# Low parts of the weights by an adding DMA on POOL, and the forget logs broadcast from device memory

## The chip, the cores and the metric

One core of one Trainium2 chip runs the whole program. The metric is the device time of the program in microseconds (us). Engines are named as the profile names them: PE is TensorE, DVE is VectorE, ACT is ScalarE, POOL is GpSimd, SP is SyncE, which here only issues DMAs. Each engine works through its own instructions in order.

## What is computed

Two layers over 512 tokens of width 1024. A layer projects the normalized input with one wide matrix, mixes the tokens by three branches of four heads (retention, gated linear attention, "forgetting" attention), joins them by gated projections, and ends with a gated feed-forward part with a short convolution. The forgetting attention adds a running sum of log forget gates to its logits:

```python
log_f = jax.nn.log_sigmoid(f_logit.astype(F32))
cum = jnp.cumsum(log_f, axis=1).transpose(0, 2, 1)
logits = jnp.einsum('bihd,bjhd->bhij', q[:, q0:q1], k[:, :q1]).astype(F32) * d ** -0.5
logits = logits + cum[:, :, q0:q1, None] - cum[:, :, None, :q1]
```

All inputs are float32. Modulation vectors (shift, scale, gate) come from `c_act @ w_ada`, a matrix of 6 x 1024 columns per layer.

## The kernel before

Activations lie transposed, features on the 128 partitions and the 512 tokens along the row, so one matmul has 128 rows of weights and 512 columns of tokens. To keep precision with the fp32r matmul type, every product is made of three matmuls (`mm3`, L238 to L241): rounded weight times rounded activation, rounded weight times the activation's low part, and the weight's low part times rounded activation.

All weights are laid out on the host in `wall`, 302 units of 128 x 1024 float32 (512 KB), in the order of use. A unit feeds 24 matmuls of 512 columns in most stages. It passes three steps: `dma_to` issues its load on SP into a tile `wr` (4 buffers, shared with the rows `ar` of `w_ada`), `prep_hi` rounds it on ACT into `wh` (L122, 5 buffers), and `prep_lo` makes the low part `wl` (5 buffers) as raw minus rounded on DVE (L131). `ahead` calls these for the units up to `depth` ahead of the one in use; `depth` is 3 or 4, and 1 inside a head group.

The order of the program on each engine is the order in which the code is written: there is no scheduler. `col_block` runs one unit; smaller work (norms of the heads, attention items) is queued as generators and advanced by `tick`, twice per unit, in PE steps and evacuation steps.

Stages that the text speaks of, with the time of the first layer:

- start: loads of `x`, the first units and the columns of `w_ada` that the first normalization needs (`ad`, 16 pairs); PE is kept busy with warm-up matmuls.
- first head group (`head_group`, not halved; 20 to 63 us): k runs over the 8 blocks of the input, one unit per k feeds 8 banks. For each k, `h_a` makes `ht` on DVE (L314) and `hhi` on ACT (L315), `h_b` makes `hlo` on DVE (L320); the modulation columns `mod` for the k after are summed on DVE (L333) and finished on POOL (L339 to L343). The matmuls are L363: `wh` by `hhi`, then `wl` by `hhi`, then `wh` by `hlo`.
- the three other head groups (at 576, 940 and 1498 us) work in halves of 256 tokens, with 6 banks; their normalization is finished while they run (`sums` with a power on POOL, L294; `spread`). They start out of `tail_blocks`, which prepares units ahead at fixed steps (`S1`, `S3`).
- projections and heads: `qk_evac` copies the banks (L510, L512), `qk_norm` normalizes them, `gates_item` makes the log forget gates, sums them up on 4 partitions (`cum`, L589) and sends them to all 128 partitions (`cumb`, L597). `fox_item` subtracts `cumb` from the scores (`fl`, L653); its matmuls are L649 (`fs`), L665 (`fT`) and L675 (`fo`).
- during the gated projections and the feed-forward part of layer 0, one `ar` load on SP and one sum on DVE (L151) accompany most units, 80 in all.

Of the kernel before, what the change touches and what calls it, by code (L numbers as in the profile page):

```python
# [7 lines left out]
F32 = mybir.dt.float32  # L8
F32R = mybir.dt.float32r
BF16 = mybir.dt.bfloat16  # L10
AF = mybir.ActivationFunctionType
ALU = mybir.AluOpType
# [13 lines left out]
S = 512  # L26
NH = 4
# [27 lines left out]
def tile_hybrid_layers(ctx: ExitStack, tc: tile.TileContext, xT, cvec, wall, wada, par, a2, cst, tabs, out):  # L55
# [5 lines left out]
    wh_p = ctx.enter_context(tc.tile_pool(name="wh", bufs=5))  # L61
    wl_p = ctx.enter_context(tc.tile_pool(name="wl", bufs=5))
    sm_p = ctx.enter_context(tc.tile_pool(name="sm", bufs=2))
    psm = ctx.enter_context(tc.tile_pool(name="psm", bufs=8 - NA, space=PS))
    psa = ctx.enter_context(tc.tile_pool(name="psa", bufs=NA, space=PS))

    V, A, G, T, Q = nc.vector, nc.scalar, nc.gpsimd, nc.tensor, nc.sync

    def slot(nm, dt=F32):
        return slots.tile([128, S], dt, tag="slot", name=nm)  # L70
# [6 lines left out]
    def free(n=1):  # L77
        live[0] -= n

    def ba(nm="ba"):  # L80
        live[0] += 1
        return psa.tile([128, S], F32, tag="a", name=nm)
# [3 lines left out]
    def cc(n):  # L86
        o, w = CC[n]
        return C[:, o:o + w]
# [3 lines left out]
    def pp(l, n, i=0, w=1):  # L92
        o, _ = PC[n]
        return P_l[l][:, o + i:o + i + w]
# [12 lines left out]
    raw, wgt = {}, {}  # L107
# [18 lines left out]
    def prep_lo(u):  # L126
        while state["lo"] < min(u, NU):
            i = state["lo"]
            hi = wgt[i][0]
            lo = wl_p.tile([128, UW], F32R, tag="wl", name="wl")  # L130
            V.tensor_tensor(lo, raw.pop(i), hi.bitcast(F32), op=ALU.subtract)  # L131
            wgt[i] = (hi, lo)
            state["lo"] += 1

    def prep_to(u):
        prep_hi(u)
        prep_lo(u)
# [210 lines left out]
    def head_group(l, sec, nm, h, half):  # L348
# [18 lines left out]
        if not half:  # L367
# [3 lines left out]
            ada0_sum(1, 1)  # L371
            prep_hi(2)
            prep_lo(1)
            ada0_sum(1, 0)
            h_b(l, sec, 0, t, h, FULL)
            for kc in range(KD):
                if kc + 1 < KD:
                    t = h_a(l, sec, kc + 1, nm.rb, h, FULL)
                    prep_hi(kc + 3)
                    prep_lo(kc + 2)  # L380
                    if kc + 2 < KD:
                        ada0_sum(kc + 2, 1)
                        ada0_sum(kc + 2, 0)
                    h_b(l, sec, kc + 1, t, h, FULL)
                mms(kc, None)
                dma_to(kc + 5)
                if kc + 4 < KD:
                    ada0_load(kc + 4)
# [83 lines left out]
    def layer(l, nm, h):  # L472
# [80 lines left out]
        def gk_evac(b, o):  # L553
            if b == 0:
                R["gk"] = [slot("gk"), slot("gk")]
                R["sml"] = sm_p.tile([128, NB, 20], F32, tag="sml", name="sml")
            A.copy(R["gk"][b // 2][:, (b % 2) * 256:(b % 2) * 256 + 256], o[:, 0:256])
            V.tensor_copy(R["sml"][:, b, :], o[:, 256:276])
            if b == NB - 1:
                queue.append((gates_item(), 1))  # L560
                queue.append((la_item(0), 1))
                queue.append((la_item(1), 1))
                for hh in range(NH):
                    for ib in range(NB):
                        queue.append((fox_item(hh, ib), 1 + ib // 2))

        def gates_item():
            yield P1
            ps = ba("smT")
            for b in range(NB):  # L570
                T.transpose(ps[0:20, b * 128:b * 128 + 128], in_=R["sml"][:, b, :], identity=cc("ident"))
            yield E_
            gl = slot("glrT")
            V.memset(gl[0:32, :], 1.0)
            V.tensor_copy(gl[0:20, :], ps[0:20, :])
            free()
            e = slot("fe")
            m = slot("fm")
            fb = pp(l, "foxb")[0:4]
            A.activation(e[0:4], gl[0:4], AF.Abs, bias=fb)  # L580
            A.activation(e[0:4], e[0:4], AF.Exp, scale=-1.0)
            A.activation(e[0:4], e[0:4], AF.Ln, bias=cc("one")[0:4])
            V.tensor_scalar(m[0:4], gl[0:4], fb, 0.0, op0=ALU.add, op1=ALU.min)
            yield E_
            R["glrT"] = gl
            V.tensor_tensor(m[0:4], m[0:4], e[0:4], op=ALU.subtract)
            V.memset(e[0:4], 1.0)
            cum = slot("cum")
            V.tensor_tensor_scan(cum[0:4], e[0:4], m[0:4], 0.0, op0=ALU.mult, op1=ALU.add)  # L589
            yield P1  # L590
            pc = ba("cumc")
            for b in range(NB):
                T.transpose(pc[:, b * 4:b * 4 + 4], in_=cum[0:4, b * 128:b * 128 + 128],
                            identity=cc("ident")[0:4, 0:4])
            cb = [slot("cumb") for _ in range(NH)]
            for hh in range(NH):
                Q.dma_start(out=cb[hh], in_=cum[hh:hh + 1, None, :].to_broadcast([1, 128, S]))  # L597
            yield E_
            R["cumc"] = sm_p.tile([128, 16], F32, tag="cumc", name="cumc")
            V.tensor_copy(R["cumc"], pc[:, 0:16])  # L600
            free()
            R["cumb"] = cb
# [403 lines left out]
    with tc.manual_schedule():  # L1006
# [24 lines left out]
        for k in range(KD):  # L1031
            square_acc(k, acc)
            if k in (K0, K1):
                i = int(k == K1)
# [172 lines left out]
```

## Time and profile before

| | before |
|---|---|
| median of three runs | 1866.81 us (1865.39 to 1867.63) |
| span of the profiled execution | 1864.4 us |
| DMA queue q1 (issued by SP) | 65290 packets, 218.57 MB, 38.5% of 16 engines' time |
| mean DMA rate | 118 GB/s |
| mean granted TensorE clock | 0.986 |

The profiled execution has no time of its own on the page besides its span; the median of the runs stands 2.4 us above it. The page gives busy time by engine, a row of 40 slices of 46.6 us with the busy share in tenths, the chain of work that ended last, groups of instructions by line (count, busy time, mean ns, then the idle time ahead of them and what ended it), and DMA issues with the time to landing. In timelines a row is start, length, engine, line, operation, output <- inputs, and in brackets the idle time before it with what ended that. A view of windows gives busy time, granted clock and DMA share in chosen stretches.

### The profile page before, as it was taken

The page shows a single profiled execution, that of the slowest core. Times are in us where ns is not written, and L with a number is a line of the kernel's source. Part 1 is how long each engine was busy: PE and PEld are TensorE (multiplying, and loading weights), DVE is VectorE, ACT ScalarE, POOL GpSimd, SP SyncE. Part 2 cuts the span into 40 slices and gives each one's busy share as a digit, 9 for nine tenths or more (in the row PEclk, how much of TensorE's full clock was granted, in tenths as well). Part 3 has the DMA queues.
Part 4 walks back from the last instruction along what each step waited for, and adds up shares of the span by engine and source line. Part 5 has one row for each costly group of instructions (what it writes and reads, how often), then busy time and mean ns, then how long its engine had stood idle before and what let it go on. Part 6 is the DMA issues. An engine that isn't in the chain of part 4 may idle for free.

```text
span 1864.4 us, 22544 instructions
## 1 busy us (share of the span) xinstructions
PE 1805.6 (97%) x8991; PEld 1508.4 (81%) x8991; DVE 1002.1 (54%) x1515; ACT 672.2 (36%) x1124; POOL 85.4 (5%) x101
## 2 busy tenths in 40 slices
PE   9995999999999999999999869999999999999999
PEld 6874878888889888888898648788888898888887
DVE  7663754565665676764257347544434466444321
ACT  4662433332333443332148334333323244333210
POOL 3210100000000000000001001000000000000000
PEclk9997999999999999999999979999999999999999
DMA  9346222345552465554223542322222233322231
GB/s 335 126 55 92 69 91 90 125 158 192 169 181 86 152 236 181 191 193 158 79 69 124 38 98 69 102 91 69 90 95 98 79 102 102 100 93 94 71 121 55
DMA packets 65395, 220.01 MB, mean 118 GB/s; under 512 B 7263, under 2 KB 7689, under 8 KB 65290
## 3 DMA queue, kind: packets, MB, share of 16 engines
q1 hardware_dynamic: 65290, 218.57, 38.5%
q8 instruction: 71, 1.16, 0.3%
q14 instruction: 34, 0.28, 0.0%
HBM read 214.34 MB, written 2.10 MB: 116 GB/s over the span
## 4 chain that ended last, share of the span: by engine, by line
PE 92%; DMA 3%; DVE 2%; SPq 2%; ACT 1%; issue 0%; POOL 0%; DVEq 0%; ACTq 0%
PE bm L239 23%; PE bm L241 23%; PE bm L240 23%; PE bm L363 4%; PE ga L363 4%; PE bm L534 3%; DMA wr<-wall 3%; PE bm L535 2%; PE bm L536 2%; SPq L597 2%; PE ro L795 1%; PE rs L783 1%; PE fs L649 1%; PE fo L675 1%; PE go L761 0%; ACT wh L122 0%
## 5 line engine op out<-in xcount | busy, mean ns | idle before, releaser
L131 DVE TENSOR_TENSOR wl<-wr,wh 128x1024 fp32r<-128x1024 f32 x302 | 368.8, 1224 | 360.3 <-ACT wh L122 360.0
L239 PE MATMUL bm<-hhi,wh 128*128 128x512 f32 x1296 | 520.3, 401 | 0.0
L241 PE MATMUL bm<-hhi,wl 128*128 128x512 f32 x1296 | 505.5, 390 | 0.0
L240 PE MATMUL bm<-hlo,wh 128*128 128x512 f32 x1296 | 504.9, 390 | 0.0
L122 ACT CAST wh<-wr 128x1024 fp32r<-128x1024 f32 x302 | 314.5, 1047 | 358.5 <-PE bm L240 232.2
L239 PEld LDWEIGHTS bm<-hhi,wh 128*128 128x128 f32 x1296 | 243.4, 188 | 54.4 <-issue 4.2
L240 PEld LDWEIGHTS bm<-hlo,wh 128*128 128x128 f32 x1296 | 243.5, 188 | 53.0 <-issue 2.9
L241 PEld LDWEIGHTS bm<-hhi,wl 128*128 128x128 f32 x1296 | 243.2, 188 | 51.9
L239 PE MATMUL bm<-fah,wh 128*128 128x512 f32 (+1 forms) x374 | 141.0, 377 | 0.0
L240 PE MATMUL bm<-fal,wh 128*128 128x512 f32 (+1 forms) x374 | 140.8, 377 | 0.0
L241 PE MATMUL bm<-fah,wl 128*128 128x512 f32 (+1 forms) x374 | 140.8, 377 | 0.0
L534 PE MATMUL bm<-wh,hhi 128*128 128x512 f32 (+1 forms) x256 | 99.7, 389 | 0.0
L151 DVE SCALAR_TENSOR_TENSOR ar<-ar,cact 128x1024 f32<-128x1024 f32 x80 | 97.5, 1218 | 0.0
L535 PE MATMUL bm<-wl,hhi 128*128 128x512 f32 (+1 forms) x256 | 95.5, 373 | 0.0
L536 PE MATMUL bm<-wh,hlo 128*128 128x512 f32 (+1 forms) x256 | 95.1, 371 | 0.0
L240 PEld LDWEIGHTS bm<-fal,wh 128*128 128x128 f32 x374 | 70.3, 188 | 13.0
L241 PEld LDWEIGHTS bm<-fah,wl 128*128 128x128 f32 x374 | 70.3, 188 | 13.0
L239 PEld LDWEIGHTS bm<-fah,wh 128*128 128x128 f32 x374 | 70.3, 188 | 12.7
L904 DVE SCALAR_TENSOR_TENSOR x<-bm,mod,x 128x512 f32<-128x512 f32 (+1 forms) x39 | 25.5, 655 | 101.3 <-PE bm L241 101.3
L942 DVE TENSOR_TENSOR fu<-fu,bm 128x512 f32<-128x512 f32 x42 | 28.9, 688 | 69.6 <-PE bm L241 59.8
L867 ACT ACTIVATE mg<-bm,der 128x512 f32<-128x512 f32 x48 | 32.9, 685 | 82.4 <-PE bm L241 82.4
L941 ACT ACTIVATE fu<-fu 128x512 f32<-128x512 f32 x44 | 27.8, 632 | 93.9 <-DVE fu L939 93.9
(213 smaller groups left out, 2406.3 us busy)
## 6 DMA issues: line engine op xcount, KB each, us to landing
wr<-wall SPq DMA_DIRECT2D x302, 512.0 KB, 3.6
ar<-wada SPq DMA_DIRECT2D x80, 512.0 KB, 3.9
ad<-wada SPq DMA_DIRECT2D x32, 256.0 KB, 6.0
x<-xT SPq DMA_DIRECT2D x8, 256.0 KB, 4.2
cumb<-cum SPq DMA_DIRECT2D x8, 256.0 KB, 30.2
dec<-tabs SPq DMA_DIRECT2D x8, 256.0 KB, 4.3
out<-x SPq DMA_DIRECT2D x8, 256.0 KB, 2.1
cos<-tabs SPq DMA_DIRECT2D x2, 256.0 KB, 4.0
```

The lines of the kernel that those rows point to most:

```text
L122: A.copy(hi, raw[i])
L131: V.tensor_tensor(lo, raw.pop(i), hi.bitcast(F32), op=ALU.subtract)
L151: V.scalar_tensor_tensor(out=r, in0=r, scalar=1.0, in1=cact, op0=ALU.mult, op1=ALU.mult, accum_out=mod[l][:, b:b + 1])
L239: T.matmul(o, lhsT=wh, rhs=ah, start=first, stop=False)
L240: T.matmul(o, lhsT=wh, rhs=al, start=False, stop=False)
L241: T.matmul(o, lhsT=wl, rhs=ah, start=False, stop=last)
L363: T.matmul(banks[f % GB][:, ts], lhsT=got[f // 8][wi][:, (f % 8) * 128:(f % 8) * 128 + 128], rhs=h[kc][hi][:, ts], start=kc == 0 and hf != ...
L534: T.matmul(o, lhsT=h[k][0][:, bs], rhs=wh[:, ws], start=k == 0, stop=False)
L535: T.matmul(o, lhsT=h[k][0][:, bs], rhs=wl[:, ws], start=False, stop=False)
L536: T.matmul(o, lhsT=h[k][1][:, bs], rhs=wh[:, ws], start=False, stop=k == KD - 1)
L597: Q.dma_start(out=cb[hh], in_=cum[hh:hh + 1, None, :].to_broadcast([1, 128, S]))
L867: A.activation(g, o, AF.Tanh, scale=0.5, bias=der[l][:, i * 8 + j:i * 8 + j + 1])
```

## The change

Two edits. The low part of a unit is no longer a subtraction on DVE: ACT writes the negated unit into the fp32r tile `wl` (which rounds it, so that the tile holds the negated rounded unit), and a DMA issued on POOL adds the raw unit, read once more from device memory, onto it. And the log forget gates are first stored to a tile in device memory by a DMA on POOL, and broadcast from there by four DMAs on POOL, where SP broadcast them from one SBUF partition each.

```diff
+    dr_p = ctx.enter_context(tc.tile_pool(name="dr", bufs=2, space=bass.MemoryType.DRAM))
...
             lo = wl_p.tile([128, UW], F32R, tag="wl", name="wl")
-            V.tensor_tensor(lo, raw.pop(i), hi.bitcast(F32), op=ALU.subtract)
+            A.activation(lo, raw.pop(i), AF.Copy, scale=-1.0)
+            G.dma_start(out=lo, in_=wall[i], accum_op=ALU.add)
...
+            cd = dr_p.tile([NH, S], F32, tag="cumd", name="cumd")
+            G.dma_start(out=cd, in_=cum[0:NH])
             cb = [slot("cumb") for _ in range(NH)]
             for hh in range(NH):
-                Q.dma_start(out=cb[hh], in_=cum[hh:hh + 1, None, :].to_broadcast([1, 128, S]))
+                G.dma_start(out=cb[hh], in_=cd[hh:hh + 1, None, :].to_broadcast([1, 128, S]))
```

Line numbers of the changed kernel are one to four higher (L131 becomes L132 and L133, L597 becomes L598 and L601). Three places show what moves on the engines that others wait for. First, POOL in the first head group, from the modulation columns of k = 1 on. Before:

```order
L339 TENSOR_TENSOR mod_82<-part 128x1
L340 TENSOR_TENSOR mod_82<-mod_82,par_80 128x1
L342 TENSOR_SCALAR mod_82<-mod_82 128x1
L343 TENSOR_TENSOR mod_82<-mod_82,par_80 128x1
L339 TENSOR_TENSOR mod_82<-part 128x1
L340 TENSOR_TENSOR mod_82<-mod_82,par_80 128x1
```

and now:

```order
L341 TENSOR_TENSOR mod_84<-part 128x1
L342 TENSOR_TENSOR mod_84<-mod_84,par_82 128x1
L344 TENSOR_SCALAR mod_84<-mod_84 128x1
L345 TENSOR_TENSOR mod_84<-mod_84,par_82 128x1
L133 DMA wl<-wall 128x1024
L341 TENSOR_TENSOR mod_84<-part 128x1
L342 TENSOR_TENSOR mod_84<-mod_84,par_82 128x1
L133 DMA wl<-wall 128x1024
L341 TENSOR_TENSOR mod_84<-part 128x1
```

The DMA of a unit's low part, which waits for ACT's negated pass, stands between the columns of one k and those of the next.

Second, ACT at the end of the first head group and behind it, where the banks are copied and the next units rounded. Before:

```order
L122 CAST wh<-wr 128x1024
L516 ACT_TABLE_LOAD
L510 COPY qk<-ga 128x512
L510 COPY qk<-bm 128x512 x3
L122 CAST wh<-wr 128x1024 x3
L479 ACTIVATE qsq<-qk 128x512
L465 CAST qsh<-qsq 128x512
```

and now:

```order
L123 CAST wh<-wr 128x1024
L132 ACTIVATE wl<-wr 128x1024 x2
L518 ACT_TABLE_LOAD
L512 COPY qk<-ga 128x512
L512 COPY qk<-bm 128x512 x3
L123 CAST wh<-wr 128x1024 x3
L132 ACTIVATE wl<-wr 128x1024 x3
L481 ACTIVATE qsq<-qk 128x512
L467 CAST qsh<-qsq 128x512
```

Three negated passes (L132) now stand behind the three roundings and ahead of the heads' squares.

Third, the queues at the forget logs in layer 0. On SP before:

```order
L114 DMA wr<-wall 128x1024 x9
L825 DMA cos<-tabs 128x512
L826 DMA sin<-tabs 128x512
L114 DMA wr<-wall 128x1024 x2
L597 DMA cumb<-cum 128x1x512 x4
L114 DMA wr<-wall 128x1024 x18
```

and on POOL now:

```order
L494 TENSOR_TENSOR qsq<-qsq,qv 128x512
L133 DMA wl<-wall 128x1024 x2
L598 DMA cumd<-cum 4x512
L601 DMA cumb<-cumd 128x1x512 x4
L133 DMA wl<-wall 128x1024 x4
L694 TENSOR_TENSOR rq<-rq,rt 128x512
```

On SP the unit loads now follow one another without the broadcasts; on POOL the store and the four broadcasts stand between the adding DMAs of two units.

## The prediction

> **What bounds the kernel now.** The page comes first: the busy times and the slices.
>
> ```profile
> span 1864.4 us, 22544 instructions
> PE 1805.6 (97%) x8991; PEld 1508.4 (81%) x8991; DVE 1002.1 (54%) x1515; ACT 672.2 (36%) x1124; POOL 85.4 (5%) x101
> PE   9995999999999999999999869999999999999999
> ```
>
> TensorE is busy in 1805.6 of 1864.4 us, so at most 58.8 us can be won from its idle time, and VectorE at 54% is not what sets the end. The idle time is not spread: the slices dip at the fourth and at the 23rd and 24th. The windows view, read second, measures these two places and the stages around them (columns: window, its length, busy us and instructions of PE, PEld, DVE, ACT, POOL, then granted clock, DMA share, GB/s).
>
> ```profile
> 20.00:66.00 46.00, 46.00 (x204) 37.91 (x203) 39.57 (x88) 16.90 (x22) 18.36 (x42) 1.00 0.67 244
> 66.00:110.00 44.00, 43.97 (x235) 37.93 (x234) 31.02 (x33) 36.60 (x62) 9.08 (x7) 1.00 0.40 132
> 130.00:170.00 40.00, 15.08 (x56) 11.32 (x55) 6.07 (x14) 4.55 (x13) 0.00 (x0) 0.68 0.90 87
> 390.00:560.00 170.00, 170.00 (x766) 141.14 (x765) 106.12 (x151) 53.53 (x79) 1.01 (x1) 1.00 0.54 178
> 606.00:885.00 279.00, 279.00 (x1257) 232.09 (x1257) 182.01 (x247) 99.39 (x124) 0.00 (x0) 1.00 0.55 185
> 1040.00:1100.00 60.00, 35.42 (x154) 27.23 (x153) 18.46 (x35) 16.89 (x34) 0.00 (x0) 0.80 0.72 68
> ```
>
> Idle in the two dips: 40 - 15.08 = 24.9 and 60 - 35.42 = 24.6, together **49.5 us** of the 58.8. The granted clock falls there too. The chain of waits and the timelines say who is late, once in each layer; this is layer 0.
>
> ```profile
> 131.06 9.73 SPq L597
> 140.88 24.10 DMA wr<-wall
> 135.05 0.35 DVE L653 SCALAR_TENSOR_TENSOR fl<-fs,cumc,cumb 128x128 f32<-128x128 f32 x1 [7.41 <-DMA cumb<-cum]
> 165.00 1.04 ACT L122 CAST wh<-wr 128x1024 fp32r<-128x1024 f32 x1 [25.92 <-DMA wr<-wall]
> 166.60 0.90 PE L665 MATMUL fT<-cst,fl 128*128 128x128 f32 x3 [19.34 <-ACT lae L635]
> wr<-wall SPq DMA_DIRECT2D x302, 512.0 KB, 3.6
> cumb<-cum SPq DMA_DIRECT2D x8, 256.0 KB, 30.2
> ```
>
> The four broadcasts of the forget logs (L597) each read one partition of SBUF and land after 30.2 us at the median. VectorE waits 7.41 us for the first. The weight unit issued behind them lands after 24.1 us instead of 3.6; ScalarE, which works in order, waits 25.92 us for it, and TensorE 19.34 us for what stands behind that. Outside these dips TensorE goes at its own rate, which two rows give:
>
> ```profile
> 61.57 0.68 PE ga L363 x3
> 62.25 1.13 PE bm L363 x5
> ```
>
> Eight matmuls of 512 columns take 1.81 us, a unit of 24 takes **5.44 us**. There a change shows only where a weight part comes later than TensorE asks for it.
>
> **The change, part by part.**
>
> *Broadcasts.* The log goes to device memory (one DMA) and comes back by four DMAs with 128 rows to write, issued on POOL. SP keeps nothing of it. The rows nearest to the new transfers:
>
> ```profile
> out<-x SPq DMA_DIRECT2D x8, 256.0 KB, 2.1
> dec<-tabs SPq DMA_DIRECT2D x8, 256.0 KB, 4.3
> L294 POOL TENSOR_TENSOR r<-v,cst 128x2 f32<-128x2 f32 x6 | 5.1, 851 | 716.9 <-DVE v L293 716.9
> L114 SPq DMA_DIRECT2D wr<-wall x302: 327/328/9688, 9.3 to 1832.0; - x151
> 122.98 17.81 SPq L597 DMA_DIRECT2D cumb<-cum  x4
> 130.00:135.00 5.00, 0.86 (x4) 0.41 (x3) 0.00 (x0) 0.00 (x0) 0.00 (x0) 0.95 0.92 27
> ```
>
> Store 2.1, load 4.3, and one issue on POOL before each. POOL's price of an issue is in no row: SP's is 0.33 us (327 ns at least) below, and the 9.73 us of L597 above; a small POOL operation costs 0.85, which is nearest, and I take 1.0. From 122.9 (log ready, issue of L597) the first broadcast lands at 122.9 + 1 + 2.1 + 1 + 3.3 to 4.3, about 131, against 135.05. TensorE has run dry at about 131 before (0.86 of 5 us busy from 130), so some 1.5 us of waiting stays in each layer, 3 together (0, up to 2 x 7.4 if it lands as late as now). Gain: 49.5 - 3 = 46.5. The clock adds to it:
>
> ```profile
> 135.00:140.00 5.00, 4.54 (x15) 3.96 (x16) 2.27 (x8) 2.33 (x8) 0.00 (x0) 0.50 0.88 26
> 170.00:175.00 5.00, 5.00 (x18) 3.77 (x17) 2.60 (x5) 2.79 (x8) 0.00 (x0) 0.80 0.02 9
> 1060.00:1065.00 5.00, 5.00 (x22) 4.09 (x21) 0.16 (x1) 1.20 (x4) 0.00 (x0) 0.71 0.90 27
> 1090.00:1095.00 5.00, 4.35 (x11) 2.87 (x12) 3.93 (x9) 1.99 (x6) 0.00 (x0) 0.64 0.37 118
> ```
>
> Busy time times missing clock: 2.3 + 1.0 + 1.5 + 1.6 = 6.4 us, some 8 with the windows between. **Gain 54.5 us** (about 40 to 58).
>
> *Low parts, throughput.* For each of 302 units VectorE loses a subtraction, ScalarE gets a second pass, and POOL and the DMA engines get a transfer that reads the unit and the tile and writes the tile.
>
> ```profile
> L131 DVE TENSOR_TENSOR wl<-wr,wh 128x1024 fp32r<-128x1024 f32 x302 | 368.8, 1224 | 360.3 <-ACT wh L122 360.0
> L122 ACT CAST wh<-wr 128x1024 fp32r<-128x1024 f32 x302 | 314.5, 1047 | 358.5 <-PE bm L240 232.2
> 1085.00:1090.00 5.00, 0.90 (x3) 0.50 (x3) 1.76 (x3) 1.61 (x3) 0.00 (x0) 0.50 0.99 404
> ```
>
> VectorE falls to 1002 - 369 = 633 us: worth nothing, TensorE hid it. ScalarE rises by 302 x 1.05 = 316 to 988 us, 53%, hidden behind TensorE except where it is full: 66 to 110 us, 36.6 of 44 busy, where eight more passes make 45, and the same operations in layer 1. I charge 2 us a layer, **4** (0 to 10). The DMA engines moved 404 GB/s when full, 1.30 us for 0.524 MB; a transfer that reads twice I price at 2.6. The densest stage, 606 to 885, runs 185 of 404 GB/s, 46%; 2.6 of 5.44 adds 48%: it just fits. I charge **5** (0 to 35, see the rivals).
>
> *Low parts, latency.* What was ScalarE then VectorE, 1.3 us from rounded part to low part, becomes: negated pass 1.05 us, then issue and landing. Unit loads land in 3.6 us, a second read adds 1.3: I take 5.0 from the issue on (3.6 below; 8 above, a queue of one more transfer). The lead of three to four units, over 16 us, covers that wherever units are prepared well ahead. It does not at three kinds of place.
>
> The Trainium skill, "DMA: Bandwidth & Descriptors", "Anatomy of one DMA — SWDGE (gpsimd) path", fits 2.0 us plus the bytes at 436 GB/s for a transfer issued on POOL. By it a plain unit takes 3.2, with a second read 4.4 as an estimate; the sum would be about 4 us lower. No row here shows such a transfer.
>
> First head group. Rows before, where `mod` is made on POOL for the next k:
>
> ```profile
> 25.12 0.58 POOL L339 TENSOR_TENSOR mod<-part 128x1 f32<-128x1 f32 x1 [2.39 <-DVE ad L333]
> 27.08 0.19 POOL L343 TENSOR_TENSOR mod<-mod,par 128x1 f32<-128x1 f32 x1
> 27.30 0.75 DVE L314 SCALAR_TENSOR_TENSOR ht<-x,mod,rb 128x512 f32<-128x512 f32 x1 [0.38 <-POOL mod L343]
> 28.15 0.72 ACT L315 ACTIVATE hhi<-ht,mod 128x512 fp32r<-128x512 f32 x1 [3.71 <-POOL mod L340]
> 32.69 0.75 DVE L314 SCALAR_TENSOR_TENSOR ht<-x,mod,rb 128x512 f32<-128x512 f32 x1 [0.38 <-POOL mod L343]
> ```
>
> One step takes 32.69 - 27.30 = 5.39 us, just TensorE's 5.44. Afterwards POOL stands between `ht` of k and `mod` of k+1 with the DMA of low part k, and that waits for ScalarE: `hhi` is done 1.5 us after `ht` starts, rounded part 2.55, negated part 3.6, issue 4.6, then the chain L339 to L343 (25.12 to 27.27, 2.15): 6.75 us a step. `ht` of k = 2 starts at 27.3 + 2.5 for two issues ahead of it, that of k = 7 five steps on at 63.6, its low part lands 3.6 + 5.0 later, at 72.2, and 16 matmuls (3.6) end the group at 75.8, against 62.25 + 1.13 = 63.4. Cost 12.4, and the engines are already 67% busy there: **13** (7 to 21; an issue of 2 us gives the top).
>
> After it. ScalarE rounds three units in a row, and the negated passes now stand behind all three:
>
> ```profile
> 63.98 2.97 ACT L122 CAST wh<-wr 128x1024 fp32r<-128x1024 f32 x3
> 63.22 0.47 PE L534 MATMUL bm<-wh,hhi 128*128 128x512 f32 x1
> ```
>
> First negated part 66.95 + 1.0, landed at 72.9. TensorE wants it one unit after 63.2, at 69: 3.9 us late, likewise in layer 1: **8** (4 to 14).
>
> Half head groups, three of them. The third unit is prepared only while the first is in use:
>
> ```profile
> 579.34 1.03 ACT L122 CAST wh<-wr 128x1024 fp32r<-128x1024 f32 x1
> 583.01 0.52 PE L363 MATMUL bm<-hhi,wl 128*128 128x256 f32 x3
> ```
>
> Rounded 580.4, negated 581.4, landed 586.4; wanted about 583.4 (last two of the three matmuls). 3 us each, **9** (4 to 18). New stops of 3 to 5 us cost clock as the dips do: **5** (0 to 10).
>
> The sum against the profiled execution: -54.5 + 4 + 5 + 13 + 8 + 9 + 5 = -10.5, span 1853.9. The median of the runs, 1866.81, lies 2.4 above the span; with the same around it the time is **1856 us**, 0.6% faster.
>
> **The rivals.**
>
> (1) *The DMA engines become the bound* (slower). Where a second stream (`ar<-wada`) runs, 0.55 of the engines' time is taken at 185 GB/s: 1.56 us for a unit, so by shares an adding transfer of twice that, 3.1, takes 57%, 1.12 in all. It decides from 0.45 x 5.44 = 2.4 us of all engines' time per adding transfer. 0.12 x 5.44 = 0.65 us for each of some 82 units (279 us, and the 170 from 390 on) is 54, less two leads of about 10: 35 more than I charge at least, **1890**, and up to 1910. For it: the share. Against: the 404 GB/s row, which shows the share to be no ceiling.
> By the Trainium skill, "Collectives: The Full Stack", "The bandwidth ceiling: the fold count and why AG ≠ RS ≠ AR", an add inside the transfer is bound by its two source reads (a measured ratio of 1.93 to a plain copy). That is the doubling used here; no row shows an adding transfer.
>
> (2) *The adding transfer is much dearer*, say 5 us of engine time: (1.56 + 5) / 5.44 = 1.2 of a unit everywhere, +20% of 1800, above **2100**. It starts at 3.9 us. Nothing in the trace speaks for it or against it.
>
> (3) *Quick landing*: 3.6 us from the issue on, issue under 0.5, ScalarE's gaps enough. Then the costs are near the lower ends, 7 + 4 + 4 and little else: -54.5 + 20, **1832**. For it: median landing 3.6 under load; against: two reads.
>
> (4) *The dips stay*: the broadcasts come as late as now, since POOL, in order, waits for the log's store and for adding DMAs ahead of it. Then only the costs: 1856 + 54, **1910**. The queue ahead holds one DMA whose input is ready by then, so this is unlikely.
>
> **How the numbers follow.** Forecast 0.52 (own range 1838 to 1880), rival 1 0.18, rival 2 0.07, rival 3 0.18, rival 4 0.05. About 0.2%, 3.7 us, is what a measurement can tell from no change: below 1863.1 is faster, above 1870.5 slower. Of the forecast's 0.52, 0.34 is faster, 0.09 same, 0.09 slower, by the ends of its terms. Faster 0.34 + 0.18 = 0.52; same 0.09; slower 0.09 + 0.18 + 0.07 + 0.05 = 0.39. The range goes from 1828, just under rival 3, to 1935, over rivals 1 and 4 and the upper ends together; left out are rival 2 and the outer ends, under 0.2.
>
> **What would show it.** Right: the dips at slices 4, 23 and 24 gone; `wr<-wall` landing at 24 us nowhere; ScalarE near 988, VectorE near 633 us; the first head group ending near 76 instead of 63.4; TensorE waiting 3 to 4 us for `wl` at each later group. The step on throughput fails if TensorE waits for `wl` or `wr` in the middle of 606 to 885 with DMA share near 1; the price of an issue fails if POOL's DMAs take far from 1 us; the broadcast step fails if VectorE still waits 7 us at L653. What would make it wrong most: an adding transfer that is not two plain reads.

## The result and the profile after

The changed kernel takes **1891.76 us** (median of four runs, 1888.96 to 1896.12) against 1866.2 before: ratio 1.0137 (95% interval 1.0121 to 1.0152). It is 1.4% slower; 0.6% faster was forecast. The page of the changed kernel (span, busy times, TensorE's slices, granted clock):

```profile
span 1891.7 us, 22995 instructions
PE 1820.0 (96%) x8991; PEld 1517.7 (80%) x8991; DVE 652.2 (34%) x1213; ACT 955.6 (51%) x1426; POOL 346.9 (18%) x413
PE   6899999999998999999988999999999989999999
PEclk8899999999999999999998999999999999999999
```

The dips of before are gone from their slices, and new, shallower ones stand at the start, in the 13th, the 21st and 22nd and the 33rd slice: the four head groups. VectorE and ScalarE came out near the forecast (633 and 988 expected). The windows view shows the same (columns: window, length, busy us and instructions of PE, PEld, DVE, ACT, POOL, then granted clock, DMA share, GB/s).

```profile
20.00:66.00 46.00, 35.26 (x144) 28.63 (x143) 25.84 (x67) 21.03 (x24) 19.65 (x48) 0.85 1.02 308
66.00:110.00 44.00, 34.68 (x133) 27.46 (x132) 8.36 (x15) 23.27 (x33) 8.25 (x9) 0.84 0.71 170
130.00:170.00 40.00, 36.23 (x175) 29.25 (x175) 16.93 (x32) 28.28 (x47) 11.91 (x14) 0.96 0.84 189
606.00:885.00 279.00, 271.69 (x1252) 225.86 (x1251) 119.23 (x188) 140.67 (x167) 41.64 (x49) 0.99 0.96 263
960.00:1040.00 80.00, 64.72 (x410) 59.28 (x409) 22.05 (x45) 41.74 (x61) 13.02 (x14) 0.89 0.62 139
1040.00:1100.00 60.00, 58.63 (x306) 49.22 (x306) 26.01 (x41) 46.35 (x72) 19.17 (x21) 1.00 0.89 206
```

From 20 to 66 us, where TensorE was never idle before, 10.7 us are idle now, from 66 to 110 another 9.3, and the clock falls to 0.85; the long stage 606 to 885, where the DMA engines are now 96% busy, has only 7.3 us idle. Whom TensorE waits for stands in its waits (engine, line waited for: us in total, times, longest).

```profile
PE bm L243 <- DMA wl<-wall: 18.8, 8, 8.8
PE bm L365 <- DMA wl<-wall: 17.4, 4, 6.4
PE ga L365 <- DMA wl<-wall: 14.6, 4, 10.7
PE bm L537 <- DMA wl<-wall: 7.3, 1, 7.3
PE lan L636 <- DVE fl L657: 4.0, 2, 3.5
```

And the DMA view (queue: packets, MB, share of the time of 16 engines; then transfers with the median us from issue to landing):

```profile
q0 software_dynamic: 44192, 160.47, 47.1%
wr<-wall SPq DMA_DIRECT2D x302, 512.0 KB, 6.2
wl<-wall POOLq DMA_DIRECT2D x302, 512.0 KB, 8.1
...
cumd<-cum POOLq DMA_DIRECT2D x2, 8.0 KB, 7.0
```

Of 71.7 us idle (1891.7 - 1820.0) 58.1 are **17 waits for a low part**; 302 such transfers are made, so nearly all come in time. They land after 8.1 us, not 5.0, and the units' own loads after 6.2 instead of 3.6. Both traces hold the same 8991 matmuls in the same order; the start of the n-th in the one less that in the other shows where time goes:

| matmul | before | after | behind by |
|---|---|---|---|
| first with a low part, first head group | 21.5 | 31.3 | +9.8 |
| last k of that group | 59.6 | 74.4 | +14.8 |
| first low part behind that group (L537) | 69.0 | 93.1 | +24.1 |
| behind the dip of layer 0 | 171.6 | 175.3 | +3.6 |
| first low part behind the second head group (L243) | 618.1 | 633.3 | +15.2 |
| first low part behind the third head group (L243) | 982.3 | 1021.3 | +39.0 |
| behind the dip of layer 1 | 1093.7 | 1108.8 | +15.1 |
| first low part behind the fourth head group (L243) | 1540.0 | 1565.0 | +25.0 |

The dips give back what was forecast; the group seams take more than that. Behind a stop the matmuls themselves are slower, which the timeline of TensorE shows at five of the waits:

```profile
31.30 1.65 PE L365 MATMUL ga<-hhi,wl 128*128 128x512 f32 x3 [10.74 <-DMA wl<-wall]
...
74.44 1.34 PE L365 MATMUL ga<-hhi,wl 128*128 128x512 f32 x3 [1.99 <-DMA wl<-wall]
...
85.36 0.39 PE L536 MATMUL bm<-wh,hhi 128*128 128x512 f32 x1
93.08 0.80 PE L537 MATMUL bm<-wl,hhi 128*128 128x512 f32 x1 [7.33 <-DMA wl<-wall]
...
97.52 0.63 PE L538 MATMUL bm<-wh,hlo 128*128 128x512 f32 x1
...
98.78 0.39 PE L536 MATMUL bm<-wh,hhi 128*128 128x512 f32 x1
...
633.31 0.50 PE L243 MATMUL bm<-hhi,wl 128*128 128x512 f32 x1 [3.65 <-DMA wl<-wall]
...
635.37 0.63 PE L241 MATMUL bm<-hhi,wh 128*128 128x512 f32 x1
...
1564.98 0.50 PE L243 MATMUL bm<-hhi,wl 128*128 128x512 f32 x1 [2.78 <-DMA wl<-wall]
...
1566.90 0.63 PE L241 MATMUL bm<-hhi,wh 128*128 128x512 f32 x1
```

After a stop of 7.33 us a matmul takes 0.63 instead of 0.39 us, and matmuls start 0.43 us apart instead of 0.23, for 5.7 us (93.08 to 98.78). After shorter stops the slow time comes later: behind the stop of 3.65 us the first matmuls run on, and then the granted clock is 0.81, 0.50, 0.50, 0.50 and 0.98 in the five microseconds from 634. One of these from the windows view:

```profile
636.00:637.00 1.00, 1.00 (x4) 0.79 (x3) 0.96 (x2) 0.00 (x0) 0.00 (x0) 0.50 1.08 225
```

Twice the missing clock gives 3.4 us at half clock. The stops of 2.78 us (0.73, 0.50, 0.50 and 0.56 from 1566) and of 1.99 us (0.92, 0.50, 0.50, 0.50 and 0.87 from 74) give 3.4 us as well; behind the stop of 1.70 us that ends at 730.13 the clock stays at 1.00.

### The profile page after: what moved, and what is told of

It reads as the page before. It is cut to its first block, busy times and chain, and to the rows that moved or that the text cites. A ratio compares the mean times of both kernels' runs of the same rounds, so it can differ in the third digit from the quotient of the medians.

```text
span 1891.7 us, 22995 instructions
## 1 busy us (share of the span) xinstructions
PE 1820.0 (96%) x8991; PEld 1517.7 (80%) x8991; DVE 652.2 (34%) x1213; ACT 955.6 (51%) x1426; POOL 346.9 (18%) x413
## 4 chain that ended last, share of the span: by engine, by line
PE 71%; issue 15%; DMA 8%; ACT 3%; POOL 3%; DVE 0%; SPq 0%; POOLq 0%; DVEq 0%; ACTq 0%
PE bm L243 19%; PE bm L241 19%; PE bm L242 19%; DMA wl<-wall 4%; POOL wl L133 2%; DMA ad<-wada 2%; PE bm L536 2%; PE bm L537 2%; PE bm L538 2%; PE bm L365 2%; PE ga L365 2%; PE ro L799 1%; PE fo L679 1%; PE rs L787 1%; PE fs L653 1%
## 5 line engine op out<-in xcount | busy, mean ns | idle before, releaser
L243 PE MATMUL bm<-hhi,wl 128*128 128x512 f32 x1296 | 508.7, 393 | 18.4 <-DMA wl<-wall 18.4
L133 POOL DMA_DIRECT2D wl<-wall x302 | 263.2, 871 | 1332.5 <-ACT wl L132 1240.6
L132 ACT ACTIVATE wl<-wr 128x1024 fp32r<-128x1024 f32 x302 | 318.0, 1056 | 0.0
L243 PEld LDWEIGHTS bm<-hhi,wl 128*128 128x128 f32 x1296 | 244.5, 189 | 73.5 <-DMA wl<-wall 21.3
L243 PE MATMUL bm<-fah,wl 128*128 128x512 f32 (+1 forms) x374 | 140.9, 377 | 0.4 <-DMA wl<-wall 0.4
L537 PE MATMUL bm<-wl,hhi 128*128 128x512 f32 (+1 forms) x256 | 95.2, 372 | 7.3 <-DMA wl<-wall 7.3
L941 DVE SCALAR_TENSOR_TENSOR fu<-bm,par,fu 128x511 f32<-128x511 f32 x40 | 30.0, 750 | 171.1 <-ACT fu L940 171.1
L243 PEld LDWEIGHTS bm<-fah,wl 128*128 128x128 f32 x374 | 70.4, 188 | 13.8 <-DMA wl<-wall 0.9
L894 DVE SCALAR_TENSOR_TENSOR mg<-mg,bm 128x512 f32<-128x512 f32 x32 | 21.9, 686 | 141.5 <-PE bm L243 131.6
```

The lines of the kernel that those rows point to most:

```text
L132: A.activation(lo, raw.pop(i), AF.Copy, scale=-1.0)
L133: G.dma_start(out=lo, in_=wall[i], accum_op=ALU.add)
L243: T.matmul(o, lhsT=wl, rhs=ah, start=False, stop=last)
L537: T.matmul(o, lhsT=h[k][0][:, bs], rhs=wl[:, ws], start=False, stop=False)
L941: V.scalar_tensor_tensor(out=t[:, 1:S], in0=pu[:, 0:S - 1], scalar=pp(l, "cw1", j), in1=t[:, 1:S], op0=ALU.mult, op1=ALU.add)
```

## Experiments

Theory S, from these traces: the loss stands at the seams of the four head groups, where units are prepared less than three ahead of their use and 8.1 us from issue to landing come to light. Its rivals: the two edits disturb each other (I), or the adding transfers cost by their number, through the DMA engines or ScalarE (E). The expectations call the later theories by letters of their own. Line numbers below are those of each kernel.

**The two edits apart.** The first kernel has the broadcasts through device memory, with the subtraction put back; the second has the adding transfers, with the broadcasts put back.

```diff
@@ broadcasts alone
-            A.activation(lo, raw.pop(i), AF.Copy, scale=-1.0)
-            G.dma_start(out=lo, in_=wall[i], accum_op=ALU.add)
+            V.tensor_tensor(lo, raw.pop(i), hi.bitcast(F32), op=ALU.subtract)
@@ low parts alone
-            G.dma_start(out=cd, in_=cum[0:NH])
...
-                G.dma_start(out=cb[hh], in_=cd[hh:hh + 1, None, :].to_broadcast([1, 128, S]))
+                Q.dma_start(out=cb[hh], in_=cum[hh:hh + 1, None, :].to_broadcast([1, 128, S]))
```

> Low parts by VectorE as before; only the forget logs go through device memory. Theory S (the changed kernel lost its gain at the group seams, through the 8.1 us from issue to landing of the adding transfer): the broadcasts alone win what the aligned traces give them, 26.9 + 28 = 55 us, time 1811 us (1806 to 1817). Theory I (the two edits help each other: the broadcasts can only win where VectorE and the queues have been relieved of the subtractions): less than 45 us won, above 1822 us.

> Low parts by the adding transfer, broadcasts from SBUF on SP as before. Theory S, parts that add: the kernel before plus all costs, 1866 + 82 = 1948 us (1935 to 1955). Theory I: the adding transfers meet the slow broadcasts on the DMA engines, so the dips get longer than 25 us each and the time lies above 1960 us; or the dips hide part of the costs, below 1935 us.

Broadcasts alone: **1806.43 us**, ratio 0.9676 (0.9662 to 0.9691), the fastest kernel of this study. Low parts alone: 1944.82, ratio 1.0421 (1.0405 to 1.0437). So the broadcasts win 60 us, more than either theory gave, and the low parts cost 78, within the range of S. The page of the first:

```profile
span 1802.0 us, 22557 instructions
PE 1792.2 (99%) x8991; PEld 1501.2 (83%) x8991; DVE 1002.0 (56%) x1515; ACT 672.7 (37%) x1124; POOL 91.1 (5%) x111
```

TensorE is idle for 9.8 us of the whole span.

**Which units.** A low part is made on VectorE if its unit is prepared less than three ahead of the one in use, else by the adding transfer; the second kernel has the converse (`>= 3`). The rule picks 37 units of 302, all at the four seams.

```diff
-            A.activation(lo, raw.pop(i), AF.Copy, scale=-1.0)
-            G.dma_start(out=lo, in_=wall[i], accum_op=ALU.add)
+            if i - cur[0] < 3:
+                V.tensor_tensor(lo, raw.pop(i), hi.bitcast(F32), op=ALU.subtract)
+            else:
+                A.activation(lo, raw.pop(i), AF.Copy, scale=-1.0)
+                G.dma_start(out=lo, in_=wall[i], accum_op=ALU.add)
```

> The changed kernel, but 37 of the 302 low parts, those prepared less than three units ahead of their use (first head group, half head groups, the units right behind them), are subtracted on VectorE; 265 stay adding transfers. Theory S (latency at the seams): only the costs away from the seams stay, 2 for ScalarE and 5 for the engines' room, and the clock comes back: 1811 + 7 = 1818 us (1811 to 1828). Theory E (the adding transfers cost by their number, through the DMA engines, HBM or ScalarE): 265/302 of 82 us stay, 1883 us.

> The converse: only those 37 low parts are adding transfers, the other 265 are subtracted on VectorE. Theory S: nearly the whole cost is there, 1811 + 75 = 1886 us (1872 to 1890; somewhat less where the DMA engines are freer and the landing quicker). Theory E: 37/302 of 82 us, 1821 us.

With 265 adding transfers away from the seams 1825.92 us, ratio 0.9778 (0.9762 to 0.9794); with the 37 at the seams alone 1875.06, ratio 1.0048 (1.0030 to 1.0067). Against the broadcasts alone that is 19.5 us for 265 transfers and **68.6 us for 37**, together 88, where the changed kernel lies 85 above it. Theory S holds, E falls; but S gave 7 for the 265, and 19.5 came. Waits of TensorE, first in the kernel with 265, then in that with 37:

```profile
PE bm L246 <- DMA wl<-wall: 9.7, 6, 3.3
PE lan L639 <- DVE fl L660: 3.8, 2, 3.0
```

```profile
PE bm L246 <- DMA wl<-wall: 16.2, 3, 8.9
PE bm L368 <- DMA wl<-wall: 15.3, 3, 5.9
PE ga L368 <- DMA wl<-wall: 13.5, 4, 10.6
PE bm L540 <- DMA wl<-wall: 8.5, 1, 8.5
```

37 transfers bring 11 waits of 53.5 us, nearly those of the changed kernel.

**What the 8.1 us are made of.** Three kernels start from the one with the 37. One copies instead of adding, so that the low parts of these units are left out and only its time counts; one holds each transfer back on POOL; one holds the next units' loads back until the transfer has landed.

```diff
@@ plain copy
-                G.dma_start(out=lo, in_=wall[i], accum_op=ALU.add)
+                G.dma_start(out=lo, in_=wall[i])
@@ held back on POOL
+                G.tensor_scalar(lo, lo.bitcast(F32), 1.0, None, op0=ALU.mult)
                 G.dma_start(out=lo, in_=wall[i], accum_op=ALU.add)
@@ loads held back
                 G.dma_start(out=lo, in_=wall[i], accum_op=ALU.add)
+                if i > 10:
+                    hold = dr_p.tile([1, 8], F32, tag="hold", name="hold")
+                    Q.dma_start(out=hold, in_=lo[0:1, 0:8].bitcast(F32))
```

> The kernel with adding transfers for the 37 seam units alone, and these copy the unit over the negated part instead of adding it: the low parts of these units are left out, the raw unit stands in their place. Everything waits as before, only the second read is gone. Theory P (the path through POOL makes most of the 8.1 us: 0.9 issue, 1.7 until the first packet, 0.3 behind the last, and the rest is transfer, shared with the next unit's load): landing falls by 1.5 to 2 us to about 6.3, a dozen waits and followers get that much shorter, 1875 - 20 = 1855 us (1846 to 1863). Theory A (adding is what is slow): landing near the 3.6 to 4.5 us of a load on SP, most of the 69 us gone, 1825 to 1838 us.

> Adding transfers for the 37 seam units alone, each one held back on POOL by a multiplication of the negated part by 1.0 (128x1024, an estimate of 2 to 2.6 us from the 1.29 us of 128x512 on POOL). Theory S: time grows by a fixed rate with the time from negated part to landing. The kernels with adding and with plain transfers give that rate: (1875.1 - 1843.6) / (8.1 - 4.8) = 9.5 us for each us. So 1875 + 2.3 x 9.5 = 1897 us (1890 to 1906). If the waits are set by something that the latency does not move (DMA engines, loads): 1875 to 1880 us.

> Adding transfers for the 37 seam units alone; behind each of the 26 that come after the first head group SP stores 32 bytes of the finished low part to device memory, so that the loads behind that store are not issued before the adding transfer has landed. Theory N (the next unit's load, released by the negated pass, runs into the adding transfer): landing falls from about 8 to 5.6-6.3 us in these places. Behind the first head group the plain copies saved 48.0 - 22.2 = 25.8 us for 3.4 us of landing, 7.6 for each, so 2 us are worth 15: 1875 - 15 = 1860 us (1854 to 1867). Theory A (the adding transfer is slow by itself): landing 7.5 us and more, 1872 to 1885 us.

Plain copy: 1843.59 us, ratio 0.9878 (0.9863 to 0.9893), between the two forecasts: landing fell by 3.3 us, not by 2, and 31 of the 69 us came back. Held back on POOL: 1910.38, ratio 1.0235 (1.0220 to 1.0250). Loads held back: 1894.62, ratio 1.0148 (1.0133 to 1.0164). The landings from the DMA views of four kernels, in this order: with the 37, plain copy, held back on POOL, loads held back.

```profile
wl<-wall POOLq DMA_DIRECT2D x37, 512.0 KB, 8.1
```

```profile
wl<-wall POOLq DMA_DIRECT2D x37, 512.0 KB, 4.8
```

```profile
wl<-wall POOLq DMA_DIRECT2D x37, 512.0 KB, 5.6
```

```profile
wl<-wall POOLq DMA_DIRECT2D x37, 512.0 KB, 5.5
```

Behind the first head group an adding transfer by itself lands after about 5.5 us; it takes about 8 when the next unit's load runs beside it. And that load starts with it because the same negated pass that lets the adding transfer go also frees the raw buffer, as SP's waits in the kernel with the 37 show:

```profile
SPq L115 <- ACT wl L135: 192.0, 28, 20.0
```

One transfer each, the first at 568.4 to 575.7 with the 37 and the second at 567.3 to 572.8 with loads held back (queue: packets, MB, share of 16 engines in that window):

```profile
q0 software_dynamic: 144, 0.52, 39.7%
q1 hardware_dynamic: 144, 0.52, 25.5%
```

```profile
q0 software_dynamic: 144, 0.52, 59.7%
```

In the second no packet of SP's queue is under way. Three transfers of the kernel with loads held back that still met a load (issued at 581.85, 966.08 and 1517.43) took 7.4, 6.1 and 7.5 us. Theory N is right about the landing, and its time is wrong: 15 us faster was expected, 20 slower came, because the loads that were held are missed next. ScalarE's waits for raw units, with the 37 and with loads held back:

```profile
ACT wh L123 <- DMA wr<-wall: 34.1, 9, 7.0
```

```profile
ACT wh L123 <- DMA wr<-wall: 121.8, 30, 10.2
```

The kernel held back on POOL misses its forecast (1897) in another way. There too most transfers in the half head groups meet little or no load and land early, so that landing and delay, 5.6 + 2.9, are near the old 8.1; 18 of the 31 us that its span is longer than with the 37 are lost by the last step of the first head group, where POOL also makes `mod` for the next step:

```profile
32.30 0.90 POOL L137 DMA_DIRECT2D wl<-wall  x1 [0.31 <-POOL wl L136]
37.88 2.95 POOL L136 TENSOR_SCALAR wl<-wl 128x1024 fp32r<-128x1024 f32 x1 [2.76 <-ACT wl L135]
41.13 0.91 POOL L137 DMA_DIRECT2D wl<-wall  x1 [0.30 <-POOL wl L136]
```

A step takes 8.83 us (32.30 to 41.13). In the changed kernel it is 5.76, from the timeline of POOL:

```profile
32.71 0.89 POOL L133 DMA_DIRECT2D wl<-wall  x1 [2.96 <-ACT wl L132]
38.47 0.89 POOL L133 DMA_DIRECT2D wl<-wall  x1 [2.96 <-ACT wl L132]
```

So the chain through POOL exists as predicted, at 5.76 us a step and not 6.75. It costs little there: TensorE's own steps in that group stay at 5.44 us (five of them from 39.65 to 66.85), since it starts 9.8 us late.

**Where the first head group loses.** Only the low part of the very first unit is made on VectorE (`if i == 0` in the diff above).

> The changed kernel, but the low part of the very first unit is subtracted on VectorE. Theory F (the first head group loses its time at the landing of that one low part, for which TensorE waits 10.7 us): 8 to 11 us come back, 1892 - 9.5 = 1882 us (1879 to 1885). Theory C (as predicted: the chain of steps through POOL, with a low part landing at the end of each, sets the end of the group): the steps stay, at most 3 us come back, 1889 to 1894 us.

1886.42 us, ratio 1.0104 (1.0089 to 1.0119): 5.3 under the changed kernel's first median and 2.9 under its second (below), between the theories. TensorE no longer stops at the first unit, but at the second:

```profile
34.24 1.65 PE L368 MATMUL ga<-hhi,wl 128*128 128x512 f32 x3 [8.00 <-DMA wl<-wall]
```

The wait of 10.74 us is paid once for the whole group and moves to the next adding transfer if its first is taken away.

**Order and lead.** All low parts are adding transfers. First, each negated pass stands right behind its rounding; second, the half head groups prepare two units ahead; third, both together with the log's store and broadcasts on SP.

```diff
@@ order
-        prep_hi(u)
-        prep_lo(u)
+        for v in range(state["lo"] + 1, u + 1):
+            prep_hi(v)
+            prep_lo(v)
@@ lead
-        depth[0] = 1
+        depth[0] = 2 if half else 1
```

> The changed kernel, but where several units are prepared at once each negated pass stands right behind its own rounding on ScalarE, not behind all roundings. Theory S: the first low part behind each of the four head groups gets 2 us earlier, 1892 - 8 = 1884 us (1879 to 1888). If the order on ScalarE counts for nothing (the landing alone does): 1892 us (1889 to 1895).

> The changed kernel, but within the three half head groups units are prepared two ahead instead of one. Theory S: the half head groups lost 27.7 us and the feed-forward units behind them 10.4 to lows that come one unit too late; with one more unit of lead most of the first and part of the second goes: 1892 - 25 = 1867 us (1860 to 1875). If the five buffers hold the extra unit back, or the price is that of the transfers themselves: 1888 to 1895 us.

> The changed kernel with negated passes right behind their roundings, two units of lead in the half head groups and store and broadcasts on SP; every low part is still an adding transfer. Theory S: the three gains add up as far as they lie at different places: 1892 - 10 - 25 - 7 = 1850 us (1843 to 1865). If they overlap: 1865 to 1875 us.

Order: 1881.44 us, ratio 1.0081 (1.0055 to 1.0106), 10 us won where 8 were expected. Lead: 1880.15, ratio 1.0064 (1.0047 to 1.0081), 12 won and not 25; why half stayed is open. All three: 1867.26, ratio 1.0007 (0.9994 to 1.0020), 24 won; that is not the 1850 of gains that add up, but lies in the range for gains that overlap. Against the second median of the changed kernel (1889.30, below) the three won 8, 9 and 22. Preparing earlier takes the loss away bit by bit without touching the transfer, as S says; it brings the kernel back to before, not to the 1806 of the broadcasts alone.

**Broadcasts: source or queue.** Two edits of the broadcasts, with subtracted low parts: through device memory on SP, and straight from SBUF on POOL.

```diff
@@ device memory, on SP
-            G.dma_start(out=cd, in_=cum[0:NH])
+            Q.dma_start(out=cd, in_=cum[0:NH])
-                G.dma_start(out=cb[hh], in_=cd[hh:hh + 1, None, :].to_broadcast([1, 128, S]))
+                Q.dma_start(out=cb[hh], in_=cd[hh:hh + 1, None, :].to_broadcast([1, 128, S]))
@@ SBUF, on POOL
-                Q.dma_start(out=cb[hh], in_=cum[hh:hh + 1, None, :].to_broadcast([1, 128, S]))
+                G.dma_start(out=cb[hh], in_=cum[hh:hh + 1, None, :].to_broadcast([1, 128, S]))
```

> Broadcasts alone, through device memory, but store and broadcasts issued on SP as the broadcasts from SBUF were. Theory Src (reading one partition of SBUF was the harm): the gain stays, 1806 us (1803 to 1812, SP stands still for the store's landing, some 5 us, which the units loaded ahead cover). Theory Q (holding SP's queue was the harm): most of it goes, above 1835 us.

> Broadcasts from one partition of SBUF as before, but issued on POOL, so that SP is free. Theory Src: the transfers keep the 16 DMA engines for 25 to 30 us as before and the units' loads wait in the engines; VectorE still waits 7 us and more: 1850 to 1867 us. Theory Q: SP issues its loads in time and the dips go: 1806 to 1820 us.

Device memory on SP: 1807.12 us, ratio 0.9685 (0.9670 to 0.9699), as on POOL. SBUF on POOL: 1823.91, ratio 0.9776 (0.9761 to 0.9790), outside both ranges and much nearer to that of Q. With a quick source the queue does not matter, but with the slow one it does: moving the broadcasts to a queue without loads behind them wins 43 of the 60 us although each still takes 26 us. The last 17 are the source's: VectorE still waits 21.2 us for the broadcasts, and TensorE 9.3 behind it. From the DMA view of the kernel with SBUF on POOL:

```profile
cumb<-cum POOLq DMA_DIRECT2D x8, 256.0 KB, 26.4
```

**The two edits together.** The separate effects add up to 1806.4 + 1944.8 - 1866.6 = 1884.6; the changed kernel lay 7 us above. Store and broadcasts were moved to SP (the first diff of the paragraph before), twice, the second time beside the changed kernel again.

> The changed kernel with the log's store and broadcasts on SP instead of POOL. The two edits together are 7 us slower than their separate results add up to (1806.4 + 1944.8 - 1866.6 = 1884.6 against 1892.0), and the store landed after 7.0 us in the changed kernel against 1.8 with the broadcasts alone. Theory R (store and broadcasts stand behind adding transfers in POOL's DMA queue): the 7 us come back, 1885 us (1882 to 1888). Theory E (the engines are simply busier): no change, 1889 to 1895 us.

> The changed kernel with store and broadcasts on SP once more, in five rounds. Theory R (POOL's queue costs the 7 us): 7 us under the changed kernel of this call, 1885 us. Theory E (the engines are busier): within 3 us of it.

> The changed kernel itself in five rounds, for comparison with the run before it and for the spread of its times: 1892 us by all theories (1888 to 1896).

On SP 1885.09 us (1882.63 to 1892.16) and again 1886.22 (1881.54 to 1887.97), ratios 1.0105 (1.0084 to 1.0126) and 1.0100 (1.0085 to 1.0115); the changed kernel beside the second 1889.30 (1886.68 to 1895.78), ratio 1.0132 (1.0112 to 1.0152). The traces show that the store's landing is at fault, as R says: with store and broadcasts on POOL the first broadcasts wait 13.5 us for it in the two layers together and TensorE waits 4.0 us behind `fl` (13.6 and 4.1 in the second trace); on SP it is 2.2 us in both traces, and TensorE has no such wait. How much of these 4 us reaches the total stays open: the intervals touch, and most kernels full of adding transfers scatter by 4 to 12 us where the kernel before scatters by 3.

## Why the prediction was wrong

The sum in four parts, from spans and busy times of three pages (before, broadcasts alone, changed); what lengthens the matmuls is counted as clock:

| part | predicted | measured | from |
|---|---|---|---|
| broadcasts, idle time | -46.5 | -49.0 | idle 58.8 to 9.8 |
| broadcasts, clock | -8 | -13.4 | busy 1805.6 to 1792.2 |
| low parts, idle time | 4 + 5 + 13 + 8 + 9 = 39 | +61.9 | idle 9.8 to 71.7 |
| low parts, clock | 5 | +27.8 | busy 1792.2 to 1820.0 |

- *Broadcasts*: the mechanism was right and the size low: 62.4 us from the spans against 54.5, over the upper end of 58, and more than half of the difference is clock. In the changed kernel the log's store, taken at 2.1 us, landed after 7.0 among adding transfers. VectorE waits 8.0 us for a broadcast in layer 0, which the prediction named as a sign against this step; TensorE waits 4.0 us in both layers, where 3 were priced.
- *Throughput of the low parts*: right in the main, priced too low. The adding queue takes 0.471 x 1891.7 / 302 = 2.95 us of all engines for a transfer (2.6 predicted), and TensorE stays nearly full from 606 to 885; by the prediction's own sign the step fails a little, since TensorE waits for `wl` three times in the middle of that stage (at 673.73, 730.13 and 818.31), 2.9 us in all. For ScalarE and the engines together 4 + 5 were priced, and the kernel with 265 transfers away from the seams lost 19.5. **Rival 1** gave 1890, and the time came out there by chance: its stage lost 7 us, and its reading of the share 0.55 as a ceiling is refuted by 0.96 with TensorE at work in 271.7 of 279 us.
- *Latency of the low parts*: here it failed. **The step is "I take 5.0 from the issue on (3.6 below; 8 above, a queue of one more transfer)".** The transfer alone takes 5.5, so the estimate from its bytes was sound; but the case at the upper bound is the rule, since most adding transfers run beside the load that their own negated pass has released. Measured: 8.1 at the median. With 8.1 in place of 5.0 the prediction's own sums come near: 3 + 3.1 = 6.1 us in each half head group, where single waits of 5.24, 6.43 and 5.33 were measured, and 3.9 + 3.1 = 7.0 behind the first head group, where it was 7.33.
- *Places of the latency*: the first head group cost 14.8 against 13, but this agreement is luck: the prediction had it from steps of 6.75 us and put the first low part at nothing, while the steps stayed at 5.44 and 9.8 of the 14.8 us come at that first low part. Behind it 9.3 came (14.8 to 24.1) where 4 was priced. In the half head groups 9 was priced, and TensorE waited 19.3 (17.4 + 14.6 of L365, less 10.74 and 1.99 in the first group). Behind these three groups 4 was priced, for layer 1 alone; L243 shows 18.8 us in 8 waits, 15.2 of them at the three places of the table (3.65, 8.8 and 2.78). The places behind the second and the fourth head group were put at nothing.
- *Clock*: 5 was charged for stops of 3 to 5 us. The stops are up to 10.7 us, there are more of them, and the clock falls behind those of 2 to 4 us as well.

The Trainium skill, "TensorE: Matmul & The Clock Gate", "Part 1: The HAM clock gate", says that the array's clock is halved after an idle window of about 3.4 us and comes back after as much sustained work. The trace agrees on the way back (3.4 us at half clock behind three of the stops) and differs on the stop: 2.78 and 1.99 us of waiting, less than that window, were followed by half clock too, and only 1.70 us were not. So here a stop of 2 us already cost another 1.7 us of missing clock.

By the Trainium skill, "DMA: Bandwidth & Descriptors", "Anatomy of one DMA — SWDGE (gpsimd) path", an adding transfer was estimated at 4.4 us; alone it took 5.5, and a plain copy, beside a load, 4.8 instead of 3.2. The fit has no term for a transfer beside it, and that term was the larger one here: 2.6 us (5.5 to 8.1) against 1.1 (4.4 to 5.5).

Would 5.0 have saved the forecast? With plain copies, which land at 4.8, the 37 seam units cost 37 us (1843.6 - 1806.4), the other 265 cost 19.5: 1806.4 + 56.7 = 1863, an estimate, as it takes the two as adding up. A plain copy also holds the engines for less time (its queue takes 3.3% of the span against 6.2% with adding), which this does not part from the landing. By the estimate some 29 of the 36 us that the forecast missed are the adding transfer's, and the unpriced seams and the clock leave the rest: the changed kernel would have been near even.

## What to carry to other kernels

A step that goes from a compute engine to a DMA is priced by time from issue to landing at the places with the least lead, and one asks what else the same event releases: here the load that shares the engines with it. Count every place where lead falls to one or two units, not only those where the first wait is seen; 37 of 302 units carried 80% of the cost. When a change has two edits that touch different resources, price and try them apart: one of these two is worth 3.2%, and the other takes it away.

## What was not expected of the hardware

Broadcasting 1 MB from single SBUF partitions holds all 16 DMA engines ten times as long as from device memory. The first row is from the kernel before, 122 to 160 us, the second from the kernel with the broadcasts alone, 118 to 135 us (with the small store):

```profile
q1 hardware_dynamic: 523, 0.97, 85.4%
```

```profile
q0 software_dynamic: 352, 1.06, 18.2%
```

0.854 x 38 = 32.5 us against 0.182 x 17 = 3.1.

An adding transfer suffers from a load beside it, 8.1 against 5.5 us, while a plain copy on the same queue landed at 4.8 with the load in the same place, as the window 567.5 to 572.2 of the kernel with plain copies shows:

```profile
q1 hardware_dynamic: 144, 0.52, 35.0%
q0 software_dynamic: 144, 0.52, 30.4%
```

How long a plain copy takes with no load beside it was not measured, and why the adding one suffers so much is open.
